# Moving the loads of a streaming kernel from SyncE's queue to GpSimd's software queue

## The chip, the cores and the metric

The kernel runs on one core of a Trainium2 chip. The metric is device time in microseconds (us) of that core, the median of several executions. The other cores were idle.

Some names: TensorE does matmuls (PE in the profile; PEld is its weight loading, which overlaps), VectorE is DVE, ScalarE is ACT, GpSimd is POOL, SyncE is SP. Sixteen DMA engines move all data between DRAM and on-chip memory. A descriptor names one contiguous piece of data to move, and the trace calls such a move a packet (65,536 packets of 8 KB for the loads and stores before). The descriptors of one queue that wait on one engine are called its ring here. The profile calls the queues that SyncE and ScalarE issue to "hardware_dynamic" and GpSimd's "software_dynamic": for each load that it issued, GpSimd itself was busy for 0.59 us.

## The reference, cut to what matters

```python
# x: (64, 1024, 1024) f32, route_w: (1024, 16), experts: (16, 64, 64)
best_head = np.argmax(x @ route_w, axis=-1)
x_heads = x.reshape(B, S, 16, 64)
for h in range(16):
    out[:, :, h, :] = (x_heads[:, :, h, :] @ experts[h]) * (best_head == h)[:, :, None]
```

The kernel reads 268 MB, writes 268 MB, and does little arithmetic for each byte.

## The kernel before

The 65,536 tokens are taken in 256 pairs of 128-token tiles. A pair is 1 MB in and 1 MB out. Each of the 128 partitions holds two consecutive tokens, 8 KB that are contiguous on both sides. TensorE transposes the tile (16 transposes a pair, line L115), multiplies five of the eight 128-column blocks in a "split pass" of 64x64 pieces (L136; 80 weight loads and 80 matmuls a pair), and the other three as whole blocks (L150). ScalarE copies results out (`raw`, `xt`), VectorE finds the best head and multiplies, GpSimd multiplies the rest, and SyncE stores.

```python
WAYS = 2; XIN_BUFS = 10; OUT_BUFS = 6; XT_BUFS = 5; AHEAD = 7
ORDER = "TTTTFTFTFTTFTFTFTTTTTT"       # T: a transpose, F: a whole block
...                                    # constants are loaded by nc.scalar.dma_start
    def load(g):
        xin = xin_pool.tile([P, 2, D], FP32, name="xin", tag="xin")
        for r in range(WAYS):          # even partitions, odd partitions: 512 KB each
            nc.sync.dma_start(out=xin[r::WAYS], in_=xg[g, r::WAYS])
        return xin
...
    for j in range(-2 * AHEAD, NT + 2, 2):
        if j + 2 * AHEAD < NT:
            xins[j + 2 * AHEAD] = load(j // 2 + AHEAD)     # 7 pairs ahead
        ...
        for i in pair:
            work[i] = split_pass(xts[i])
        ...                            # transposes of pair j mixed with whole blocks of pair j-2
                finish(ot[:, i % 2, :], ps_w, *work.pop(i))
                ...
                    for r in range(WAYS):
                        nc.sync.dma_start(out=og[i // 2, r::WAYS], in_=ot[r::WAYS])
```

## Time and profile before

| | before |
|---|---|
| median of 3 runs | 1344.7 us (1339.88 to 1344.74) |
| profiled run | 1338.1 us |
| TensorE busy | 96% |
| data queue's packets, share of 16 DMA engines | 98.6% |
| GpSimd busy | 54% |

The first lines are from the page of the kernel before: the span; busy time of each engine (us, share of the span, instructions); DMA queues (packets, MB, share of 16 engines); the chain of work that ended last, by engine; and DMA issues (count, KB each, median us from issue to landing).

```profile
span 1338.1 us, 66342 instructions
PE 1290.3 (96%) x27648; PEld 1208.3 (90%) x27648; DVE 933.7 (70%) x4098; ACT 923.2 (69%) x1537; POOL 721.9 (54%) x1031
...
q1 hardware_dynamic: 81920, 536.94, 98.6%
q8 instruction: 218, 3.57, 1.0%
...
DMA 96%; PE 1%; SPq 0%; DVE 0%; issue 0%; POOL 0%; ACT 0%; ACTq 0%; POOLq 0%; DVEq 0%
...
xin<-in_x_dram SPq DMA_DIRECT2D x512, 512.0 KB, 10.2
out_dram<-ot SPq DMA_DIRECT2D x512, 512.0 KB, 10.2
...
mv<-in_route_w_dram ACTq DMA_DIRECT2D x1, 16.0 KB, 3.2
```

The DMA engines look full, and the chain that ended last is almost all DMA. TensorE is at 96%, so it cannot be far behind.

Part of TensorE's timeline before (start us, length us, and what) shows the undisturbed beat: a split pass begins every 4.92 to 4.93 us.

```profile
703.24 1.61 PE L136 MATMUL ps_s<-mv,xt 64*64 64x80 f32 x80
...
708.16 1.61 PE L136 MATMUL ps_s<-mv,xt 64*64 64x80 f32 x80
...
713.09 1.61 PE L136 MATMUL ps_s<-mv,xt 64*64 64x80 f32 x80
```

### The profile page before, as it was taken

How to read it: one execution, taken by the hardware profiler on the slowest of the kernel's cores; microseconds unless marked ns; L12 is line 12 of the kernel's file. 1: busy time of each engine (PE TensorE's matmuls, PEld its weight loads, DVE VectorE, ACT ScalarE, POOL GpSimd, SP SyncE). 2: the span in 40 equal slices, each digit the busy share in tenths (PEclk: the TensorE clock that was granted, in tenths of full speed). 3: DMA queues.
4: the chain of work that ended last, by engine and by line, in shares of the span. 5: the costliest groups of instructions: out<-in, count | busy, mean ns of one | idle time of the engine just before them, and what ended most of it. 6: DMA issues, size and time to landing. Idle time of an engine off the chain costs nothing.

```text
span 1338.1 us, 66342 instructions
## 1 busy us (share of the span) xinstructions
PE 1290.3 (96%) x27648; PEld 1208.3 (90%) x27648; DVE 933.7 (70%) x4098; ACT 923.2 (69%) x1537; POOL 721.9 (54%) x1031
## 2 busy tenths in 40 slices
PE   7999999999999999999999999999999999999995
PEld 7888998999998999999998999889998999999995
DVE  4666766677776777777777677667777777767775
ACT  5666766767766777777676776667766767767673
POOL 3455555555555555555555555555555555555554
PEclk9999999999999999999999999999999999999998
DMA  8999999999999999999999999999999999999997
GB/s 340 421 421 416 413 407 409 407 407 406 412 398 377 418 417 399 395 412 414 398 393 404 410 416 418 402 408 397 410 407 410 412 407 417 416 405 416 417 409 327
DMA packets 84412, 541.51 MB, mean 405 GB/s; under 512 B 18576, under 2 KB 18576, under 8 KB 18576
## 3 DMA queue, kind: packets, MB, share of 16 engines
q1 hardware_dynamic: 81920, 536.94, 98.6%
q8 instruction: 218, 3.57, 1.0%
q10 hardware_dynamic: 2192, 0.33, 0.1%
q14 instruction: 82, 0.67, 0.1%
HBM read 268.76 MB, written 268.44 MB: 401 GB/s over the span
## 4 chain that ended last, share of the span: by engine, by line
DMA 96%; PE 1%; SPq 0%; DVE 0%; issue 0%; POOL 0%; ACT 0%; ACTq 0%; POOLq 0%; DVEq 0%
DMA out_dram<-ot 95%; DMA xin<-in_x_dram 1%; SPq L106 0%; PE ps_w L150 0%; PE ps_t L115 0%; DMA mv<-in_route_w_dram 0%; PE ps_s L136 0%; POOL ot L181 0%; DVE ot L173 0%; ACTq L88 0%; ACT raw L143 0%; ACT xt L117 0%; DVE mask L164 0%; POOLq L249 0%; DVE lg L158 0%
## 5 line engine op out<-in xcount | busy, mean ns | idle before, releaser
L181 POOL TENSOR_TENSOR ot<-raw,mask 128x384 f32<-128x384 f32 (+1 forms) x1024 | 721.2, 725 | 605.6 <-ACT xt L117 338.0
L117 ACT COPY xt<-ps_t 128x512 f32<-128x512 f32 x1024 | 576.7, 589 | 288.5 <-PE ps_t L115 288.0
L115 PE MATMUL ps_t<-ident,xin 128*128 128x128 f32 x4096 | 756.5, 277 | 9.7 <-DMA xin<-in_x_dram 6.9
L150 PE MATMUL ps_w<-mf,xt 128*128 128x144 f32 x3072 | 580.3, 289 | 1.5 <-DVE ot L173 1.1
L115 PEld LDWEIGHTS ps_t<-ident,xin 128*128 128x128 f32 x4096 | 499.7, 141 | 33.6 <-issue 8.9
L150 PEld LDWEIGHTS ps_w<-mf,xt 128*128 128x128 f32 x3072 | 464.2, 191 | 8.8 <-DVE ot L173 6.3
L136 PE MATMUL ps_s<-mv,xt 64*64 64x80 f32 x20480 | 430.0, 232 | 22.6 <-issue 21.9
L136 PEld LDWEIGHTS ps_s<-mv,xt 64*64 64x64 f32 x20480 | 381.1, 133 | 73.2 <-issue 62.8
L143 ACT COPY raw<-ps_s 128x704 f32<-128x704 f32 x512 | 371.1, 747 | 104.3 <-PE ps_s L136 64.9
L173 DVE TENSOR_TENSOR ot<-ps_w,mask 128x384 f32<-128x384 f32 x512 | 285.6, 558 | 98.5 <-DMA out_dram<-ot 83.8
L127 DVE TENSOR_REDUCE lgs<-ps_s 128x16 f32<-128x96 f32 x512 | 121.4, 251 | 106.3 <-ACT raw L143 105.4
L164 DVE TENSOR_SCALAR mask<-hid,ix 128x16 f32<-128x16 f32 x512 | 120.0, 234 | 56.0 <-POOL ot L181 0.9
L124 DVE TENSOR_REDUCE lgw<-ps_w 128x16 f32<-128x48 f32 x512 | 103.3, 202 | 78.9 <-PE ps_w L150 78.1
L158 DVE TENSOR_TENSOR lg<-lgs,lgw 128x16 f32<-128x16 f32 x512 | 131.8, 257 | 17.6
L160 DVE MAX8 mx<-lg 128x8 f32<-128x16 f32 x512 | 91.2, 178 | 17.6
L162 DVE FIND_INDEX8 ix<-mx,lg 128x8 uint32<-128x16 f32 x512 | 86.5, 169 | 0.0
L162 DVE MATCH_VALUE_LOAD ix<-mx,lg 128x8 f32 x512 | 47.2, 92 | 17.7
L117 ACT ACT_TABLE_LOAD x1 | 1.3, 1283 | 7.3 <-DMA mf<-in_experts_dram 7.3
L81 DVE MEMSET mf<- 128x432 f32 x1 | 0.4, 418 | 0.9 <-PEq L238 0.9
masks.py:197 POOL MEMSET ident<- 128x128 f32 x1 | 0.2, 205 | 0.3 <-POOLq L238 0.3
masks.py:199 POOL TENSOR_SCALAR_AFFINE_SELECT ident<-ident 128x128 f32<-128x128 f32 x1 | 0.3, 294 | 0.0
L238 POOL MEMSET const-float32-0.0<- 128x1 f32 x1 | 0.1, 99 | 0.2 <-issue 0.2
(5 smaller groups left out, 0.6 us busy)
## 6 DMA issues: line engine op xcount, KB each, us to landing
xin<-in_x_dram SPq DMA_DIRECT2D x512, 512.0 KB, 10.2
out_dram<-ot SPq DMA_DIRECT2D x512, 512.0 KB, 10.2
mv<-in_experts_dram ACTq DMA_DIRECT2D x2, 48.0 KB, 4.7
mf<-in_experts_dram ACTq DMA_DIRECT2D x2, 48.0 KB, 2.4
mv<-in_experts_dram ACTq DMA_DIRECT2D x2, 32.0 KB, 3.9
mv<-in_route_w_dram ACTq DMA_DIRECT2D x1, 24.0 KB, 4.6
mf<-in_route_w_dram ACTq DMA_DIRECT2D x1, 24.0 KB, 3.1
mv<-in_route_w_dram ACTq DMA_DIRECT2D x1, 16.0 KB, 3.2
```

What stands on the lines that cost most here:

```text
L115: nc.tensor.transpose(ps_t[:, q, :], xin[:, t, p * P:(p + 1) * P], ident)
L117: nc.scalar.copy(out=xt[:, half * (NB // 2):(half + 1) * (NB // 2), :], in_=ps_t)
L124: nc.vector.tensor_reduce(out=lg, in_=parts.rearrange("k s h -> k h s"), op=ALU.add, axis=AX.X)
L127: nc.vector.tensor_reduce(out=lg, in_=parts.rearrange("k b s h -> k h b s"), op=ALU.add, axis=AX.XY)
L136: nc.tensor.matmul(ps[th * 64:(th + 1) * 64, half, o0:o0 + W], lhsT=xt[half * 64:(half + 1) * 64, p, th * 64:(th + 1) * 64], rhs=mv[half * ...
L143: nc.scalar.copy(out=raw[:, :, 0:RW], in_=ps[:, :, 0:RW])
L150: nc.tensor.matmul(ps[:, o0:o0 + STEP], lhsT=xt[:, NS + f, :], rhs=mf[:, f, :], start=(f == 0), stop=(f == NF - 1), skip_group_check=True)
L158: nc.vector.tensor_add(out=lg, in0=lgs, in1=lgw)
L162: nc.vector.max_index(out=ix, in_max=mx, in_values=lg)
L164: nc.vector.tensor_scalar(out=mask, in0=hid, scalar1=ix[:, 0:1], scalar2=None, op0=ALU.is_equal)
L173: nc.vector.tensor_tensor(out=ov[:, NS:], in1=bc(mk[:, NS:]), op=ALU.mult, in0=ps[:, W:W + NF * STEP].rearrange("k (f w) -> k f w", w=STEP ...
L181: nc.gpsimd.tensor_tensor(out=ov[:, ab:NS:2], in0=rv4[:, 0:n, :, o0:o0 + Dh], in1=bc(mk[:, ab:NS:2]), op=ALU.mult)
```

## The change

The intent is to relieve SyncE, which issued loads and stores alternately so that one could wait behind the other, to put the loads on a queue of their own, and to use one transfer of 1 MB for each pair. Stores stay where they were.

```diff
     def load(g):
         xin = xin_pool.tile([P, 2, D], FP32, name="xin", tag="xin")
-        for r in range(WAYS):
-            nc.sync.dma_start(out=xin[r::WAYS], in_=xg[g, r::WAYS])
+        nc.gpsimd.dma_start(out=xin, in_=xg[g])
         return xin
```

## The prediction

> **What bounds it now.** The 16 DMA engines. The chain of waits that ended last is 95% stores out_dram<-ot and 1% loads; the slices show DMA at 9 throughout; the queue table gives the one data queue 98.6% of the 16 engines' span. The DMA packet records say how that time is made up: 65,536 data packets of 8 KB, most of exactly 309 ns (26.5 GB/s an engine, 424 GB/s on 16), so 1,266 us per engine at that floor; another 45 us are packets that took longer, up to 2.7 us; 16,384 semaphore packets of 9 ns cost 9 us; instruction fetch costs 13 us. The sum is 1,333 of 1,338 us. One pair (1 MB in, 1 MB out) takes 5.2 us.
>
> TensorE is close behind. Undisturbed, its period in the timeline is 4.93 us per pair (split passes beginning at 703.24, 708.16, 713.09), or 1,261 us for 256 pairs; with about 25 us of head and tail it could not go below some 1,285. So no change of queues can gain more than about 4%.
>
> **What the change does.**
> - It removes 512 load issues of 0.51 us from SyncE, and SyncE's 336 us of waits in front of loads. Neither is on the chain: the engines stay full behind them. Worth about 0.
> - It removes 256 of 1,024 transfers, so about 4,096 of the 16,384 semaphore packets, if a large transfer still ends with one per engine: 2.3 us per engine.
> - The bytes stay, and so does the 309 ns floor if packets stay at 8 KB (a partition's 8 KB is contiguous on both sides).
> - It adds 256 descriptor generations to GpSimd. The Trainium skill, "DMA: Bandwidth & Descriptors", section "Specifications", puts software first-byte latency at about 1 us; taking this as my estimate of the Pool time, GpSimd goes from 722 to about 980 us (54% to 73%). Per pair that is 2.8 + 1.0 of 5.2 us: it fits into the idle 605 us before its multiplies. Loads run 7 pairs (36 us) ahead, so loads queued behind multiplies aren't late.
> - It moves loads to a second ring. Each engine now alternates between load and store packets instead of draining one FIFO. The same skill page, section "Issuing engines are not separate DMA queues", says that this gives no more bandwidth. The backlog shifts to the stores: their median to landing goes from 10.2 to perhaps 14 us, the loads' falls below 10. Waits for out_dram stay.
> - Head: the first load leaves after GpSimd's constants and a generation, 1 to 2 us later than before; constants on ScalarE's queue now compete with fewer, larger transfers and may come some us later.
>
> What I cannot cost is whether the 45 us of slow packets shrink or grow with software rings and mixed directions; I allow -20 to +50 us.
>
> **Prediction.** 1347 us, range 1322 to 1390. Faster by over 2%: 0.08; within 2%: 0.72; slower by over 2%: 0.20.
>
> **Right if:** the data queues together still hold 97% or more of the engines; the floor packet is still 309 ns; the chain still ends in DMA for over 85%; GpSimd's busy share is 65 to 80%; TensorE has no wait for xin beyond the head over 10 us in total.
>
> **Wrong if:** software packets are smaller or slower than 309 ns per 8 KB (slower); generation takes 2.4 us or more, which makes GpSimd the limit and shows as waits of ScalarE and TensorE on ot or raw (slower); some engines are slowed by fetching descriptors, and loads wait for the slowest (slower); alternating directions removes the slow packets, and TensorE becomes the limit near 1,295 us (faster).

## More of the kernel before

The waits of the kernel before come next (who waited for whom: us in total, times, longest us). "Issue" means that the engine waited for nothing that the profile shows.

```profile
DVE ot L173 <- DMA out_dram<-ot: 83.8, 104, 1.8
POOL ot L181 <- DMA out_dram<-ot: 76.3, 40, 3.0
...
PEld ps_s L136 <- issue: 62.8, 241, 1.9
...
PE ps_s L136 <- issue: 21.9, 35, 1.8
```

VectorE and GpSimd wait for stores to free output buffers. TensorE itself waits for hardly anything but "issue".

## The result, and the profile after

After: 1393.62 us median of 3 runs (1391.69 to 1394.46). The ratio to before is 1.0373, with a 95% interval of 1.0335 to 1.0412: slower by 3.7%, just outside the predicted range. (A ratio is the mean time of one kernel's fast runs over that of the other's in the same rounds, so it is not quite the ratio of the medians.)

The same lines of the page after the change; line numbers are smaller by one:

```profile
span 1392.6 us, 66089 instructions
PE 1297.4 (93%) x27648; PEld 1215.2 (87%) x27648; DVE 932.3 (67%) x4098; ACT 923.5 (66%) x1537; POOL 856.6 (62%) x1287
...
q0 software_dynamic: 36864, 268.45, 50.8%
q1 hardware_dynamic: 40960, 268.47, 46.1%
q8 instruction: 218, 3.57, 1.0%
...
PE 92%; issue 5%; DMA 2%; ACTq 0%; ACT 0%; POOL 0%; DVE 0%; POOLq 0%; DVEq 0%
...
L105 POOL DMA_DIRECT2D xin<-in_x_dram x256 | 151.0, 590 | 5.1 <-PE ps_w L149 1.7
...
xin<-in_x_dram POOLq DMA_DIRECT2D x256, 1024.0 KB, 9.9
out_dram<-ot SPq DMA_DIRECT2D x512, 512.0 KB, 9.6
...
mv<-in_route_w_dram ACTq DMA_DIRECT2D x1, 16.0 KB, 20.2
```

Its waits:

```profile
PEld ps_s L135 <- issue: 129.5, 329, 9.7
...
PE ps_s L135 <- issue: 61.4, 73, 2.3
PE ps_s L135 <- DMA mv<-in_route_w_dram: 13.0, 2, 9.5
...
DVE ot L172 <- DMA out_dram<-ot: 1.0, 4, 0.3
```

Three things are to be seen. The chain that ended last is now TensorE and "issue", not DMA. The waits for output buffers are gone: VectorE's fell from 83.8 to 1.0 us. TensorE's waits for "issue" in the split pass doubled for the weight loads and nearly tripled for the matmuls. And at the start it waited 13 us for the constants `mv`; the last part of them landed 3.2 us after its issue before, and 20.2 us after it now.

**What "issue" is.** This is TensorE's weight loading after the change (start, length, what, count, and in brackets the idle time before):

```profile
733.48 0.89 PEld L135 LDWEIGHTS ps_s<-mv,xt 64*64 64x64 f32 x44 [0.17 <-issue]
735.41 0.75 PEld L135 LDWEIGHTS ps_s<-mv,xt 64*64 64x64 f32 x36 [1.04 <-issue]
...
739.63 1.17 PEld L135 LDWEIGHTS ps_s<-mv,xt 64*64 64x64 f32 x63 [0.17 <-issue]
741.63 0.40 PEld L135 LDWEIGHTS ps_s<-mv,xt 64*64 64x64 f32 x17 [0.83 <-issue]
```

A split pass of 80 is broken after 44, and the next after 63. Count what lies between the two breaks: 36 weight loads, then 28 of the transposes and whole blocks, then 63, so 127. Each has its matmul, which makes 254 instructions, and with two semaphore instructions 256. After the first 60 us, 41 of the 47 pauses of the weight loads over 250 ns before, and 77 of 78 after, stand at this same place in a count of 256 of TensorE's instructions (or at the next one). The Trainium skill, page "Runtime: NRT & Kernel Launch", section "Instruction fetch mechanics", says that instructions are fetched in blocks of 16 KiB, 256 instructions, over DMA, the next block while the current one runs. The trace agrees: 218 packets of 16 KB, one for nearly every block. The packet records around the two breaks, worked out from the trace:

```
TensorE enters a block    fetch packet of the next one    TensorE enters the next    pause
728.87 us                 733.17 to 734.09                735.41 (1.32 us later)     1.04 us
735.41                    739.36 to 740.32                741.63 (1.31 us later)     0.83
```

In the blocks with a pause, the next block was entered a median of 1.35 us (before) and 1.37 us (after) after its fetch packet ended. And of 209 blocks of the kernel before, none was entered less than 1.22 us after its packet's end. So TensorE was waiting for that packet. Below, these pauses of over 250 ns at this place in every 256 instructions, after the first 60 us, are called late fetches.

**Where the 54.5 us between the two profiles are.** I measured the time from one pair's split pass to the next. Undisturbed it is 4.926 us in both kernels. This table is worked out from the traces:

| us | before | after | change |
|---|---|---|---|
| start to the split pass of the third pair of tiles worked on | 21.5 | 37.1 | +15.6 |
| 253 periods of 4.926 us | 1246.3 | 1246.3 | 0 |
| excess of periods with a late fetch (45; 79) | 39.8 | 92.5 | +52.7 |
| excess of the other periods | 13.1 | 3.9 | -9.2 |
| the end | 17.4 | 12.8 | -4.6 |
| sum | 1338.1 | 1392.6 | +54.5 |

So the head accounts for some 15 us. The periods with a late fetch account for the rest; their 52.7 us are partly paid back where before waited for other things.

### The profile page after: what moved, and what is told of

Same layout as the page of the kernel before. It is cut to its first block, busy times and chain, and to the rows that moved or that the text cites. A ratio compares the mean times of both kernels' runs of the same rounds, so it can differ in the third digit from the quotient of the medians.

```text
span 1392.6 us, 66089 instructions
## 1 busy us (share of the span) xinstructions
PE 1297.4 (93%) x27648; PEld 1215.2 (87%) x27648; DVE 932.3 (67%) x4098; ACT 923.5 (66%) x1537; POOL 856.6 (62%) x1287
## 3 DMA queue, kind: packets, MB, share of 16 engines
q1 hardware_dynamic: 40960, 268.47, 46.1%
## 4 chain that ended last, share of the span: by engine, by line
PE 92%; issue 5%; DMA 2%; ACTq 0%; ACT 0%; POOL 0%; DVE 0%; POOLq 0%; DVEq 0%
PE ps_t L114 35%; PE ps_s L135 30%; PE ps_w L149 27%; DMA mf<-in_route_w_dram 2%; POOL ot L180 0%; ACT raw L142 0%; ACTq L88 0%; ACTq L92 0%; ACTq L90 0%; ACT xt L116 0%; POOLq L248 0%; DVE ot L172 0%; DVE ix L161 0%; DVE mask L163 0%; DVE lg L157 0%
## 5 line engine op out<-in xcount | busy, mean ns | idle before, releaser
L135 PE MATMUL ps_s<-mv,xt 64*64 64x80 f32 x20480 | 442.0, 233 | 76.9 <-issue 61.4
L135 PEld LDWEIGHTS ps_s<-mv,xt 64*64 64x64 f32 x20480 | 386.5, 133 | 134.0 <-issue 129.5
L126 DVE TENSOR_REDUCE lgs<-ps_s 128x16 f32<-128x96 f32 x512 | 128.8, 252 | 215.8 <-ACT raw L142 214.5
L105 POOL DMA_DIRECT2D xin<-in_x_dram x256 | 151.0, 590 | 5.1 <-PE ps_w L149 1.7
L157 DVE TENSOR_TENSOR lg<-lgs,lgw 128x16 f32<-128x16 f32 x512 | 117.5, 230 | 17.6
## 6 DMA issues: line engine op xcount, KB each, us to landing
mv<-in_route_w_dram ACTq DMA_DIRECT2D x1, 16.0 KB, 20.2
```

Source lines behind the costliest of these rows:

```text
L105: nc.gpsimd.dma_start(out=xin, in_=xg[g])
L126: nc.vector.tensor_reduce(out=lg, in_=parts.rearrange("k b s h -> k h b s"), op=ALU.add, axis=AX.XY)
L135: nc.tensor.matmul(ps[th * 64:(th + 1) * 64, half, o0:o0 + W], lhsT=xt[half * 64:(half + 1) * 64, p, th * 64:(th + 1) * 64], rhs=mv[half * ...
L157: nc.vector.tensor_add(out=lg, in0=lgs, in1=lgw)
```

## The experiments

The theory after reading the traces had two parts. First, the head: with 8 MB of software loads queued at once, the constants' small packets take turns with 8 KB packets and arrive late. Second, the steady state: fetches get through the DMA engines later and stop TensorE. The rivals were GpSimd's time for descriptors (0.59 us a pair); the size of the transfer; the second ring; the software descriptors; and a lower capacity of the DMA engines, of which late fetches would be only the symptom ("theory I" in the expectations; "theory II" is that the fetches themselves bind).

All runs in one table; medians and ratios are of fast runs (e7 had two slow runs of five besides, e13 one of four). "Late" is the sum of late fetches, in the one profiled run. "Slow" is, per DMA engine, the time that 8 KB packets took beyond the 309 ns of most of them; both are worked out from the traces. (Each ratio is to runs of before in the same rounds; their medians were 1336.8 to 1344.7 us.)

| run | median us | ratio to before | late, us | slow, us |
|---|---|---|---|---|
| before | 1344.7 | | 27.5 | 44.7 |
| after | 1393.62 | 1.037 | 75.9 | 76.1 |
| e1 first 9 pairs on SyncE | 1379.79 | 1.030 | 74.4 | 70 |
| e2 two software transfers a pair | 1393.38 | 1.040 | 76.5 | 77 |
| e3 4 KB descriptors | 1395.44 | 1.044 | 75.8 | 65 (own base of 159 ns a load packet) |
| e4 before, GpSimd kept busy | 1336.73 | 0.999 | 28.4 | 43 |
| e5 loads on ScalarE | 1371.9 | 1.028 | 27.4 | 55 |
| e6 all on GpSimd | 1420.58 | 1.061 | 71.5 | 96 |
| e7 after, split passes spread | 2037.87 | 1.525 | void | |
| e8 before, split passes spread | 2001.57 | 1.497 | void | |
| e9 after, 1/16 of stores left out | 1391.89 | 1.037 | 74.7 | 93 |
| e10 before, 1/16 left out | 1344.31 | 1.001 | 52.9 | 63 |
| e11 stores on GpSimd, loads on SyncE | 1379.9 | 1.028 | 65.2 | 64 |
| e12 before, loads of 1 MB | 1372.17 | 1.022 (1.017 to 1.027) | 67.6 | 66 |
| e13 after, load moved within the period | 1406.69 | 1.051 | 89.1 | 88 |
| e14 e13 and e1 | 1402.7 | 1.045 | 98.6 | 89 |
| e15 e5, loads later | 1387.23 | 1.034 | 46.0 | 74 |
| e16 after, half of stores left out | 1353.23 | 1.010 | 43.5 | 182 |
| e17 before, half left out | 1307.46 | 0.976 | 19.0 | 107 |
| e18 after, 3 output buffers | 1394.84 | 1.042 | 74.3 | 75 |

### e1: the head alone

```diff
+        if g < 9:
+            for r in range(WAYS):
+                nc.sync.dma_start(out=xin[r::WAYS], in_=xg[g, r::WAYS])
+        else:
+            nc.gpsimd.dma_start(out=xin, in_=xg[g])
```

> As after, but the first 9 pairs are loaded by SyncE in halves as in before; GpSimd loads from pair 9 on. Theory (head + instruction fetch): the constants no longer take turns with 8 MB of software loads, so the split passes begin near 13 us instead of 24.5, GpSimd's first multiply near 16 us instead of 31.8, and the time falls by 10 to 16 us to about 1380; TensorE's waits at instruction-block boundaries stay near 76 us in total. Rival (all of the 49 us lies in the steady state): the time stays within 4 us of 1393. Rival (software ring only matters through its head): the time returns to 1345.

Measured: 1379.79 us, 14 us less than after, with late fetches unchanged at 74.4 us. The third split pass began at 22.8 us, not 37.1. The head is settled at some 14 us; the rest is steady state. The packet records show how it came about: in after, each DMA engine served one constant packet of 64 or 256 bytes and then one 8 KB load packet, in turn, for over 20 us. In before, constants went through in groups of up to 37 packets with nothing between them.

### e2 and e3: transfer size and descriptor size in software

```diff
-        nc.gpsimd.dma_start(out=xin, in_=xg[g])
+        for r in range(WAYS):                                                  # e2
+            nc.gpsimd.dma_start(out=xin[r::WAYS], in_=xg[g, r::WAYS])
+        for t in range(2):                                                     # e3, in its place
+            nc.gpsimd.dma_start(out=xin[:, t, :], in_=xg[g, :, t, :])
```

> As after, but each pair is loaded by two GpSimd transfers of 512 KB (even, odd partitions), 8 KB descriptors as before. Theory (a load packet of 8 KB in a second ring goes before every instruction fetch packet): nothing that matters changes; within 1% of after, waits at block boundaries 65 to 90 us; GpSimd's issue time doubles from 151 to about 300 us and still fits. Rival (one transfer of 1 MB is what hurts): the time falls by over 20 us. Rival (descriptor generation on GpSimd delays the multiplies and so the release of raw): the time rises by over 20 us.

> As after, but each pair is loaded by two GpSimd transfers of one token column each: 512 KB with descriptors of 4 KB in place of 8 KB. Theory (the turn of the other ring delays instruction fetches): load packets take about 155 ns, a fetch waits less, waits at block boundaries fall from 76 to 35-60 us and the time falls by 10 to 30 us to 1365-1385. Rival (software ring slow by itself or size of transfer): same as e2 within 5 us. Rival (more descriptors cost more): slower than e2 by over 10 us.

e2 is like after, as the theory expected. Two software transfers in place of one change nothing, though GpSimd's busy share rose from 62% to 71%. For e3 the theory expected late fetches of 35 to 60 us, and they stayed at 75.8. So the length of one load packet is not what a fetch waits for, and this form of the theory fell.

### e4: GpSimd's time alone

```diff
     def load(g):
+        nc.gpsimd.memset(busy, 0.0)        # busy: 128x512, used by nobody
```

> As before (loads on SyncE), plus one dead GpSimd memset of 128x512 per pair, about 0.5 us, as much GpSimd time as a software load took (0.59 us), at the same place in its program. Theory (fetch): same as before within 0.5%; waits at block boundaries 20 to 35 us. Rival (GpSimd's descriptor time delays multiplies, raw, ps_s): slower by over 15 us, with ScalarE's waits for GpSimd above 60 us.

Measured: 0.999 of before, late fetches 28.4 us. GpSimd's busy time was 841.1 us, close to the 856.6 us of after. GpSimd's time is not the cause.

### e5 and e6: who writes the descriptors, and how many rings

```diff
-            nc.sync.dma_start(out=xin[r::WAYS], in_=xg[g, r::WAYS])
+            nc.scalar.dma_start(out=xin[r::WAYS], in_=xg[g, r::WAYS])          # e5
-                        nc.sync.dma_start(out=og[i // 2, r::WAYS], in_=ot[r::WAYS])
+                        nc.gpsimd.dma_start(out=og[i // 2, r::WAYS], in_=ot[r::WAYS])   # e6, from after
```

> As before, but the two 512 KB loads of a pair are issued by ScalarE, the stores by SyncE: a second ring for the loads, with hardware descriptors. ScalarE gets about 1 us of issuing per pair and has some 1.4 us of idle time. Theory A (two rings that take turns on every engine are what costs, by whoever writes the descriptors): waits at instruction-block boundaries above 60 us, excess of slow packets above 60 us per engine, steady rate near that of after (about 398 GB/s between 100 and 1000 us), time 1360 to 1390. Theory B (software descriptors cost, not the second ring): steady rate near 408 GB/s, waits at boundaries 20 to 40 us, time within 1% of before.

> As after, but the stores are issued by GpSimd too: one software ring holds loads and stores, SyncE issues nothing. GpSimd's issue time is about 3 x 0.59 us per pair. Theory A (two rings taking turns): steady rate back near 408 GB/s, waits at boundaries 20 to 45 us, so about 1350-1365 with the late head still there. Theory B (software descriptors): as after or slower, slow packets 70 us or more per engine, rate 398 GB/s or below.

e5 is slower than before by 2.8%, but not through fetches: they are at 27.4 us. ScalarE now issues 1 us of DMA instructions a pair, the median period rises from 4.927 to 5.119 us, and the head is late (third split pass at 35.4 us). The longer period also leaves fetches more time, so this does not clear a second ring. e6 has one ring for all data, and late fetches of 71.5 us. A second ring is therefore not needed for them. e6 has one more cost, which showed unasked: VectorE's small addition of two on-chip inputs rose from 257 to 698 ns while GpSimd was 81% busy. The Trainium skill, page "SBUF — State Buffer", section "Who interferes with whom", says that a VectorE instruction with two on-chip inputs contends with a GpSimd instruction that reads there. The trace of e6 agrees: the addition took 175 ns on the average when no multiply of GpSimd overlapped it, also in the 87 cases where only a DMA issue of GpSimd did, and over 570 ns on the average when a multiply did.

### e7 and e8: making TensorE less sensitive (void)

Since the split pass uses up instructions fastest, I spread its ten groups between transposes and whole blocks (S in the new order).

```diff
-ORDER = "TTTTFTFTFTTFTFTFTTTTTT"
+ORDER = "STTSTTSTFSTFSTFSTTSTFSTFSTTSTFTT"
```

> As after, but the ten 8-matmul groups of the split passes are spread evenly between transposes and whole blocks, so that 256 TensorE instructions last about 5.8 us everywhere in place of 5.2 to 6.9. Theory II (late instruction fetches cause the loss, the DMA engines follow): waits at boundaries fall below 30 us in total and the time falls by 25 us or more. Theory I (the DMA engines' lower rate is the cause and late fetches are only how it reaches TensorE): the waits move elsewhere (for xin or out_dram), the rate between 100 and 1000 us stays within 1% of 398 GB/s and the time stays within 10 us of after. Void if TensorE's undisturbed period per pair rises above 5.1 us from 4.93.

> As before, with the same spreading of the split passes. The DMA engines were full there (408 GB/s), so both theories expect at most 15 us of gain; waits at boundaries below 10 us from 27.5. If TensorE's period per pair rises above 5.1 us it is slower.

Both are of no use for the question. The expectation of e7 had called it void, and that of e8 slower, if the period rose above 5.1 us; it rose far above (1996.6 us over 256 pairs is 7.8 us a pair in e8). The timeline of e8 shows the cost of changing between 64x64 pieces and full-size matmuls. A group of 8 and two transposes take 0.66 us, where the undisturbed rates of the kernel before (80 in 1.61 us, 6 transposes in 0.82 us) would give about 0.43 us:

```profile
900.00 0.37 PE L136 MATMUL ps_s<-mv,xt 64*64 64x80 f32 x8
900.30 0.44 PE L115 MATMUL ps_t<-ident,xin 128*128 128x128 f32 x2
900.66 0.37 PE L136 MATMUL ps_s<-mv,xt 64*64 64x80 f32 x8
```

So no run takes the late fetches away and leaves all else alone.

### e9 and e10: 3% fewer bytes

```diff
-                    for r in range(WAYS):
+                    for r in range(WAYS) if (i // 2) % 16 != 15 else ():
```

> As after, but the stores of every 16th pair are left out (wrong result on purpose): 16.8 MB of 541 MB, worth about 42 us of the 16 engines at 398 GB/s. Theory I (the DMA engines' rate bounds after; late instruction fetches only pass it on to TensorE): the time falls by 30 to 45 us, the rate stays at 398 GB/s or so, and the waits at block boundaries shrink to make room. Theory II (late fetches bound it for their own reasons): the time falls by less than 15 us and the engines show idle time, with a rate about 3% lower.

> As before, with the same stores left out (wrong result on purpose). Bounded by the DMA engines at 408 GB/s it would gain up to 41 us, but TensorE's own floor is 21.5 + 253 x 4.926 + 14.5 = 1282 us plus late fetches: 1300 to 1315 expected by both theories; a gain under 10 us would say that the DMA engines do not bound before.

After gained nothing: it took 1391.89 us, where a DMA bound would have given a gain of 30 to 45 us, and late fetches stayed. Neither did before gain anything, where both theories had expected 25 us or more. That miss says the most: **a kernel whose DMA engines are busy for 98.6% of the span did not get faster when 16.8 MB of its 541 MB were taken away.** In e10 the waits for output buffers went away, late fetches rose from 27.5 to 52.9 us, and the time stayed. VectorE waited 0.2 us for them in all. These are e10's data queue, its chain that ended last, and TensorE's largest wait:

```profile
q1 hardware_dynamic: 79360, 520.16, 96.4%
...
PE 95%; issue 3%; ACT 0%; DMA 0%; POOL 0%; DVE 0%; ACTq 0%; POOLq 0%; DVEq 0%
...
PE ps_s L136 <- issue: 37.3, 52, 2.4
```

The chain, 96% DMA in before, is now 95% TensorE, in the same time. So the two paths were level in before: shortening the one left the other. e10 does not show that the DMA engines never held before up.

### e11 and e12: the reverse, and the size in hardware

```diff
-                        nc.sync.dma_start(out=og[i // 2, r::WAYS], in_=ot[r::WAYS])
+                        nc.gpsimd.dma_start(out=og[i // 2, r::WAYS], in_=ot[r::WAYS])   # e11, from before
-        for r in range(WAYS):
-            nc.sync.dma_start(out=xin[r::WAYS], in_=xg[g, r::WAYS])
+        nc.sync.dma_start(out=xin, in_=xg[g])                                           # e12, from before
```

> The reverse of the change: loads on SyncE as in before, stores on GpSimd in two halves. If software descriptors make packets slow in either direction, the stores (4 us of slow packets per engine in after) now show 25 us or more and the time is 1355 to 1400, with the early head of before. If only software loads are slow, the stores' packets stay below 10 us, the loads' near 45 us or below, and the time is within 1% of before.

> The size part of the change alone: as before, but each pair is loaded by one SyncE transfer of 1 MB in place of two of 512 KB. By e2 the size should not matter: within 1% of before, slow packets 40 to 50 us per engine, waits at block boundaries 20 to 35 us.

e11 is slower too (1.028), with late fetches of 65.2 us. Its slow packets are those of the hardware loads (50.5 us), not of the software stores (13.0 us), so here slow packets go with loads and not with software. Neither side of its expectation is met cleanly: the time is that of the first, and the stores' 13.0 us lie between the two. e12 missed its expectation: one transfer of 1 MB in place of two, with hardware descriptors on one queue, costs 2.2% (95% interval 1.7 to 2.7%) and brings late fetches to 67.6 us. These are TensorE's waits in e12:

```profile
PEld ps_s L135 <- issue: 108.2, 336, 1.9
...
PE ps_s L135 <- issue: 52.0, 77, 1.7
```

They are close to those of after. Software descriptors are therefore not needed for late fetches. The change contains a part, 1 MB in one transfer, that does most of the damage by itself when SyncE issues it: 33 of the 54.5 us between the profiles. But size is not tested alone there. With fewer issues SyncE also issues at other moments: the loads' median moved from 2.0 to 3.2 us after the start of a split pass. And on GpSimd the split into two does not help (e2).

### e13, e14 and e15: when the load is issued

In after, load and stores of a pair are issued in one burst, 2.9 to 3.5 us after a split pass began. In before, issues are spread over most of the period. I moved the load to 1.0 us (e13; a given load so goes out about 3.1 us later, in the next period), with the early head too (e14), and moved ScalarE's loads of e5 to 2.0 to 4.0 us (e15).

```diff
-        if j + 2 * AHEAD < NT:
+        if j + 2 * AHEAD < NT and j < 2:
             xins[j + 2 * AHEAD] = load(j // 2 + AHEAD)
 ...
                 finish(ot[:, i % 2, :], ps_w, *work.pop(i))
+                if i == pair[0] and j + 2 * AHEAD < NT:
+                    xins[j + 2 * AHEAD] = load(j // 2 + AHEAD)
```

> As after, but from the second iteration on the load is issued between the multiplies of the two tiles, at about 1.1 to 1.7 us after the start of the split passes, not with the stores at 2.5 to 3.5 us. Theory (load and stores issued in one burst delay the instruction fetches that fall behind it): waits at block boundaries fall from 76 to 25-50 us, time falls by 20 to 45 us to 1350-1373. Rival (software loads delay fetches whenever they are issued): both within 10 us of after.

> e13 and e1 together: the first 9 pairs on SyncE. Theory: e13's gain and e1's 14 us add, to 1335-1360, at best level with before. Rival: as e1, about 1380.

> As e5 (loads on ScalarE, hardware descriptors), but issued after the first tile is finished, so that they fall together with the stores at about 2.5 to 3.5 us. Theory (burst): waits at block boundaries rise from 28 us in e5 to 45-80 us. Rival (software descriptors): they stay at 20 to 35 us. The time itself may move by what ScalarE's issuing delays; the waits decide.

The burst theory fell: with load and stores apart, late fetches rose to 89.1 and 98.6 us, and e13 and e14 were slower than after and e1. e15 landed where that theory wanted it (46.0 from 27.4), but only just. What the three runs show together is weaker: the moment of issue alone moved late fetches by 13 to 24 us, upward in all three.

### e16, e17 and e18: traffic, and output buffers

```diff
-                    for r in range(WAYS):
+                    for r in range(WAYS) if (i // 2) % 2 == 0 else ():          # e16 from after, e17 from before
-OUT_BUFS = 6
+OUT_BUFS = 3                                                                    # e18, from after
```

> As after, with the stores of every second pair left out (wrong result on purpose, a quarter of all bytes less). If the late fetches come from packets ahead of them on the DMA engines, waits at block boundaries fall below 25 us from 76 and the time to 1305-1330 (37 us head, 253 x 4.926 us, about 10 us of tail, and the rest of the waits). If they come from something else (software descriptors, GpSimd), they stay above 50 us and the time above 1350.

> As before, with the same stores left out (wrong result on purpose). TensorE's floor with the early head is 21.5 + 1246 + about 10 = 1278 us; if traffic makes the late fetches, 1280 to 1300 us, with waits at block boundaries below 20 us. If they stay at 50 us as in e10, 1325 or more.

> As after, with 3 output buffers in place of 6. If before has few late fetches because waits for output buffers hold the pipeline back, then such waits return (over 30 us for out_dram on VectorE and GpSimd), waits at block boundaries fall below 55 us, and the time stays within 10 us of after or falls. If not, waits at block boundaries stay near 76 us and the new waits come on top: 1400 or more.

e16 and e17 give wrong results on purpose. With a quarter of the bytes gone, late fetches fall in both (75.9 to 43.5, and 27.5 to 19.0). So traffic is part of what makes them. But e16 missed its range (below 25 us and 1305 to 1330 us expected), and its 1353 us lie on the side of the rival; e17 was 7 us above its range. The DMA engines now have room, as the windows of e16 show (stretch in us; length; busy us of PE, PEld, DVE, ACT and POOL; TensorE's clock; DMA share; GB/s):

```profile
400.00:700.00 300.00, 292.83 (x6325) 275.38 (x6326) 214.84 (x939) 210.13 (x351) 194.97 (x292) 1.00 0.88 310
```

The same stretch of e17:

```profile
400.00:700.00 300.00, 297.86 (x6480) 281.07 (x6479) 217.06 (x960) 215.45 (x361) 168.44 (x240) 1.00 0.84 318
```

At a DMA share of 0.84 to 0.88 the loads on GpSimd still cost 46.1 us (the profiles: 1351.3 against 1305.2). Worked out as in the table above, 15.1 us of them are the head, 27.2 us the periods with a late fetch, and 3.8 us the rest. So most of the loss is there without a full DMA. A lack of DMA capacity is not needed to explain it.

e18 came out between its two cases. The waits for output buffers came back in part (10.8 us on VectorE and 24.9 on GpSimd; 83.8 and 76.3 in before), late fetches stayed at 74.3 us, and the time within 2 us of after. That speaks against the theory, but a pipeline held back as much as before's was not made. Pacing by SyncE, which in before waited 709 us for transfers to land and in after 2.9 us, does not explain it alone either: in e12 SyncE waited some 593 us, and late fetches were at 67.6 us. Why before has few late fetches stays open.

## Why the prediction was wrong, point by point

- **"What bounds it now. The 16 DMA engines."** This step failed: the prediction took the DMA engines for the path that sets the time after the change too, and there it is TensorE's path (92% of the chain). The share of 98.6% was read as a bound, and e10 shows that 3% fewer bytes gain nothing. The sum of packet times was right as arithmetic, but it is no fixed cost: the slow part rose from 44.7 to 107 us when a quarter of the bytes were taken away (e17). At the floor of 309 ns the packets of a pair need 16 x 0.309 = 4.944 us on each engine, and TensorE's beat is 4.926 us, so the two were level. The time of after is TensorE's beat plus late fetches, a head and an end. The prediction had that beat and called it "close behind", but let nothing stop TensorE.
- **"Instruction fetch costs 13 us."** It was counted as occupied engine time. What matters is when the fetch arrives. Late fetches cost 27.5 us before and 75.9 us after, and no line of the prediction allowed for them. This is the missing term, and most of the miss: periods with a late fetch cost 52.7 us more than before.
- **"Head: ... 1 to 2 us later than before; constants ... may come some us later."** The mechanism was named, the size was not: 15.6 us in the traces, 14 us in e1. The landing of 20.2 us in place of 3.2 us could have been estimated, with turns of one constant packet and one load packet: the 9 loads issued in the first 8 us are 72 packets of 309 ns on each engine, so 22 us.
- **Descriptor generation, "about 1 us", GpSimd at 73%:** 0.59 us and 62%, below the 65 to 80% named. It fits and costs nothing (e4), as predicted.
- **Slow packets, "-20 to +50 us":** +31 us, inside the band, but e16 and e17 show that this is not a price that adds to the time.
- **"Waits for out_dram stay", stores landing after 14 us:** VectorE's went from 83.8 to 1.0 us, and stores land after 9.6 us. The loads, "below 10", took 9.9 us.
- **"Right if": the chain ends in DMA for over 85%.** It is TensorE at 92%. The queues' share came to 96.9%, where 97% or more was named, and the 309 ns floor and TensorE's waits for `xin` (7.2 us, in the head) came as foretold; they just did not decide the time.

**What is shown and what stays open.** Shown: the 14 us of the head (e1); that GpSimd's time costs nothing (e4); that most of the loss remains with spare DMA capacity (e16, e17); and, by accounting in the trace, that the rest of the time goes into periods with pauses that end some 1.35 us after a fetch packet. Not shown by an experiment: that taking away the late fetches alone would give the time back, since e7 and e8 were void. Open: why a fetch gets through later with 1 MB loads or with anything on GpSimd. In the class of blocks that would last 5.3 to 5.6 us, where most late fetches are, the fetch packet began a median of 3.2 us after the block was entered in before, and 3.8 us in after; a second ring, software descriptors, the packet's length and the burst were each tried, and none explains it alone. No variant with right results beat before: e4's 0.999 is the same time.

## What to carry to other kernels

A DMA share near 100% with TensorE close behind is not a bound until a run with a few per cent fewer bytes gets faster, and such a run costs little. On a kernel with many small matmuls, count the instructions between TensorE's pauses: if they stand at one place in every 256, as here, suspect that instruction fetches arrive late behind your data, and that regrouping transfers moves them. When a queue takes over the bulk loads, see to it that small constants land before the deep prefetch begins.

## What the Trainium skill lacked or had wrong

- "Runtime: NRT & Kernel Launch", section "Instruction fetch mechanics", calls the crossing of a 16 KiB boundary mostly hidden. Here it was not: late fetches took 27.5 of 1338 us before and 75.9 of 1393 us after; TensorE paused at 41 of 210 block crossings before and at 77 of 213 after. The page does not say that fetches come later when the kernel's own data fill the DMA engines (75.9 us fell to 43.5 with a quarter of the bytes gone, e16), nor that TensorE goes on about 1.35 us after the packet's end.
- "DMA: Bandwidth & Descriptors", section "Queues, rings and completion order", gives packets of 9 to 17 descriptors as typical between changes of ring, with a ceiling of 64. Here there were fewer. In after, software and hardware ring changed after every 8 KB descriptor for over 60% of the packets; with two hardware queues (e5), 65% of the packets stood in runs of exactly 8. (The records do not name the engine; I followed engines by matching ends to starts.)
- The same page, section "Issuing engines are not separate DMA queues", says that issuing from several engines only saves issue time. It did not add bandwidth here either (386 GB/s after, 401 before). But the kernels with two issuing engines were slower, by 2.8% (e5, where ScalarE's issue time and a late head weigh most, and e11) and by 3.7% (after), and the page does not warn of that.
- The same page, sections "Bandwidth" and "Rules for kernel authors", recommends transfers of at least 1 MiB. In e12, 1 MB in place of 2 x 512 KB on the same queue was slower by 2.2% (1.7 to 2.7%).
- No page gives a cost for changing between 64x64 pieces and full-size matmuls on TensorE. Spreading ten groups a pair between others took the kernel from 1337 to 2002 us (e8). If the 18 changes a pair that this adds account for the longer pair (7.8 us in place of 4.93), one costs about 0.16 us, an estimate. The point belongs to "TensorEngine Tiling (Array Packing)".
